# Ten ungated tiles of an up projection as five pairs in seven half-width products, and four of eleven weight sums made early

## The chip, the cores and the metric

The kernel runs on one core of a Trainium2 chip. A core has a matrix engine (TensorE, PE in the profile; its weight loads are PEld), a vector engine (VectorE, DVE), a scalar engine (ScalarE, ACT), a general one (GpSimd, POOL) and a synchronisation engine (SyncE, SP). DMA queues are fed by SP, POOL and ACT. The metric is the device time of one execution in microseconds (us), as the median of several. Profiles come from one execution of their own.

## The reference

One encoder block over 512 tokens with 1024 channels, all in float32: RMS norm, one combined projection, three token mixers (a bidirectional chunkwise mLSTM, a neighbourhood attention, a cross-attention into a memory), a gated merge, an output projection, and a feed-forward part. The change touches only the last:

```python
def conv_glu_ffn(h, w_up, w_conv, b_conv, w_down):
    a, u = jnp.split(h @ w_up, 2, axis=-1)
    return (jax.nn.gelu(dwconv3(a, w_conv, b_conv)) * u) @ w_down
```

`h` is 512 x 1024, `w_up` 1024 x 5632 (2816 columns for `a`, the gated half that goes through a convolution along the tokens and a gelu, and 2816 for `u`, the ungated half) and `w_down` 2816 x 1024.

## The kernel before

**Numbers.** A float32 product is made of three: each operand is split into a high part (a rounded copy) and a low part (the rest), and TensorE adds high x high, high x low and low x high in PSUM (`mm3`, L224 to L226). Weights arrive as blocks of 1024 columns on 128 partitions (512 KB) on SP's queue into three raw buffers (`wr`), and are split in two halves of 512: ACT copies the high part (`wh`, L184), DVE subtracts it for the low part (`wl`, L185), into four buffers each. `weights(key)` asks for a block and issues loads and splits a fixed number of blocks ahead.

**The up loop.** Channels lie on partitions, tokens along the free axis. There are 22 gated tiles (`ua`, 128 channels each) and 22 ungated ones (`uu`); each is 8 x 3 matmuls of 128 x 512 (`proj`, eight slices of 128 input channels), and tile f's two follow one another. After `ua` ACT and DVE make the convolution and the gelu (L1573 to L1576; L1574 and L1575 are 511 columns on DVE), and after `uu` DVE multiplies the two into a buffer for the down projection (L1581). The tokens' operands are `HH` (high) and `HL` (low).

**The down projection** multiplies 2 x 2 blocks with seven products in place of eight (a Strassen scheme in Winograd's form, p1 to p7, in the order of `ORDER`). It needs sums of the four weight blocks. They are made for 11 slices during the up loop, by f=2, 3, 4, 6 and on up to 15 (`SUMS`): a slice of four blocks (1 MB, `wdn`) is loaded by POOL's queue (L1477), DVE adds 1024 columns (L1495) and 512 (L1483), ACT copies 1024 (L1484), DVE adds 512 (L1492) and subtracts 1024 (L1487), and POOL's queue stores the results (`tsp`, `tdn`) to DRAM, from where the down projection loads them as its weights. From f=4 on three of a slice's four steps are issued for each f. The tokens' sums and differences for the scheme are made by `early` and `operand` (differences on DVE, a high copy on ACT, a low part on DVE, 1024 columns each).

**Order.** The kernel is written in one sequence; a framework then schedules the instructions and gives each engine its own fixed order, which the engine keeps. A wait at one instruction so holds all behind it on that engine. PSUM has buffers of one bank (`mmps`) and in the later stages wide ones of two banks (`w2p`).

The middle stages (mixers, merge, output projection) are untouched. Before them stand the projections `mlq`, `mlk` and `tm`, with convolutions on DVE (L468 to L472).

Of the kernel before, what the change touches and what calls it, by code (L numbers as in the profile page):

```python
# [17 lines left out]
P = 128  # L18
S = 512
# [12 lines left out]
NU = 15  # L32
WARM = 14
# [31 lines left out]
def block_list():  # L65

    L = []
    for i in range(4):
        L.append((("mlq", i), 1024))
    for f in range(4):  # L70
        L.append((("mlk", f), 1024))
    for c in range(3):
        for h in range(8 // TMK[c]):
            L.append((("tm", c, h), TMK[c] * TMC[c]))
    for n in ("xaq", "o", "memk", "memv", "naq", "nak"):
        for f in range(4):
            L.append(((n, f), 1024))
    for br in range(3):
        for fp in range(4):
            for f in (2 * fp, 2 * fp + 1) if br < 2 else range(8 if fp == 0 else 0):  # L80
                L.append((("g", br, f), 1024))
            L.append((("br", br, fp), 1024))
    for f in range(FT):
        L.append((("ua", f), 1024))
        L.append((("uu", f), 1024))
    return L
# [9 lines left out]
BCOLS = {n: (lambda k: P) for n in ("mlk", "o", "xaq", "memk", "naq", "nak", "g", "ua", "uu")}  # L96
BCOLS.update({n: (lambda k: 512) for n in ("mlq", "memv")})
# [5 lines left out]
def hybrid_block(ctx, tc, xg, xT, xtok, memT, wflat, wout, wdn, vecs, gbias, nabias, out):  # L103
# [64 lines left out]
    def emit_split(i):  # L168
        key, n = BLOCKS[i]
        r = raws.pop(i)  # L170
# [31 lines left out]
    def weights(key):  # L202

        i, _, n = BINDEX[key]
        calls[0] += i >= BINDEX[("naq", 0)][0]
        if calls[0] % 2 and sums:
            sums.pop(0)()
        ahead_to(i + RAW_AHEAD, i + SPLIT_AHEAD)
        return split.pop(i)

    def sum_ops():
        for dst, src, more in ((T1, wout[B11], B12), (T3, wout[B12], B22), (T2, tout[T1], B22), (T4, tout[T2], B21)):
            for add in (False, True):
# [7 lines left out]
                yield one  # L221

# [1152 lines left out]
    HH, HL = [], []  # L1375
    halves_ = (slice(0, HS), slice(HS, S))
    first.close()
    w2p = ctx.enter_context(tc.tile_pool(name="w2p", bufs=2, space=bass.MemoryType.PSUM))
# [3 lines left out]

    def pair():
        w = wide()
        return [w[:, :S], w[:, S:]]
# [17 lines left out]
    def features():  # L1403
        h2 = [unit(F32R) for _ in range(4)]
# [3 lines left out]
    def turn(i):  # L1408
        banks = [mmps() for _ in range(4)] if i == 0 else pair() + pair()
# [60 lines left out]

    down_sums = []

    def sum_load(k):
        w = unit()[:, :4 * S]
        w4 = w.rearrange("p (q n) -> p q n", q=4)
        ks = slice(k * S, (k + 1) * S)
        G.dma_start(w4, wdn[:, :, ks].rearrange("q p n -> p q n"))  # L1477
        q = [w[:, i * S:(i + 1) * S] for i in range(4)]
        hl = []

        def high():
            hl.append(unit(F32R)[:, :4 * S].rearrange("p (x q n) -> p x q n", x=2, q=2))
            V.tensor_tensor(q[B22], q[B22], q[B11], op=ALU.add)  # L1483
            A.activation(hl[0][:, 0], w4[:, 1:3], AF.Copy)  # L1484

        def low():
            V.tensor_tensor(hl[0][:, 1], w4[:, 1:3], hl[0][:, 0].bitcast(F32), op=ALU.subtract)  # L1487
            for x in range(2):
                G.dma_start(tsp[:, x, :, ks].rearrange("q p n -> p q n"), hl[0][:, x])  # L1489

        def store():
            V.tensor_tensor(q[B21], q[B21], q[B22], op=ALU.add)  # L1492
            G.dma_start(tdn[:, :, ks].rearrange("q p n -> p q n"), w4[:, 0:4:3])

        down_sums.extend([lambda: V.tensor_tensor(w[:, :2 * S], w[:, S:3 * S], w[:, :2 * S], op=ALU.add), high, store, low])  # L1495


# [57 lines left out]
    SUMS = [2 + 4 * k // 3 for k in range(HF)]  # L1555
    for f in range(FT):
# [3 lines left out]
        ur = uu_[i][j // 4][:, j % 4 * S:(j % 4 + 1) * S]  # L1560
# [11 lines left out]
        c = scr()  # L1572
        A.activation(c, pa, AF.Identity, scale=vcol("ffw", FT + f), bias=vcol("ffb", f))  # L1573
        V.scalar_tensor_tensor(c[:, 1:], pa[:, :S - 1], vcol("ffw", f), c[:, 1:], op0=ALU.mult, op1=ALU.add)  # L1574
        V.scalar_tensor_tensor(c[:, :S - 1], pa[:, 1:], vcol("ffw", 2 * FT + f), c[:, :S - 1], op0=ALU.mult, op1=ALU.add)  # L1575
        A.activation(c, c, AF.Gelu_apprx_tanh)  # L1576
# [64 lines left out]
    for name in ORDER:  # L1641
        banks[name] = [mmps(), mmps()] if name in ("p6", "p3", "p4") else pair()
# [59 lines left out]
def _layout(inp):  # L1702
# [14 lines left out]
    for key, n in BLOCKS:  # L1717
# [25 lines left out]
        elif kind == "ua":  # L1743
            b = wu[:, :, key[1] * P:(key[1] + 1) * P]
        else:
            b = wu[:, :, DFF + key[1] * P:DFF + (key[1] + 1) * P]
# [52 lines left out]
```

## Time and profile before

| what | us |
|---|---|
| median of the runs (3) | 857.08 |
| lowest and highest | 856.96, 857.18 |
| the profiled execution's own time | 857.81 |
| its span, first to last instruction | 856.0 |
| PE busy | 848.5 |
| DVE busy | 622.5 |
| ACT busy | 481.2 |
| POOL busy | 133.0 |

The span is what the trace shows; the execution's own time has 1.8 us more around it. Busy time is a sum over the span, and an engine with a small share can still be late at one place. The up loop lies from about 504 to 745 us in this trace, the stage of `mlq`, `mlk` and `tm` between 5 and 60 us or so. A row of the timeline gives start, duration, engine, line, operation, output and inputs, and shape; matmuls overlap, so their pace is read from start to start.

### The profile page before, as it was taken

What the parts mean: (1) busy time and instruction counts of PE and PEld (TensorE: products, weight loads), DVE (VectorE), ACT (ScalarE), POOL (GpSimd) and SP (SyncE); (2) the same over time, 40 slices, a digit from 0 to 9 for tenths busy, and PEclk for the clock granted to TensorE, in tenths of its full rate; (3) what the DMA queues carried; (4) which work ended last, traced back from release to release, by engine and by line L of the source; (5) the groups of instructions that cost most, each with busy time, mean ns of one, the idle gap of its engine ahead of it and who ended that gap; (6) DMA issues with size and microseconds to landing.
All of it is one profiled execution on the core that took longest, in us unless ns stands there. A gap on an engine that the chain in (4) does not pass through costs nothing.

```text
span 856.0 us, 12111 instructions
## 1 busy us (share of the span) xinstructions
PE 848.5 (99%) x4175; PEld 717.3 (84%) x4175; DVE 622.5 (73%) x1277; ACT 481.2 (56%) x989; POOL 133.0 (16%) x245
## 2 busy tenths in 40 slices
PE   9999999999999999999999999999999999999996
PEld 7898889988888888888888888888888888888885
DVE  7774698987568758898769967475758666694684
ACT  7663467675446658888735764343444444463463
POOL 0101100010127561600000111030213100011101
PEclk9999999999999999999999999999999999999999
DMA  7233542495674444543452844487869672477942
GB/s 281 80 111 121 185 153 85 158 281 163 179 202 120 115 125 127 158 144 128 144 186 98 225 144 156 153 293 261 265 222 348 208 231 99 135 258 258 380 161 100
DMA packets 53982, 155.00 MB, mean 181 GB/s; under 512 B 6872, under 2 KB 11992, under 8 KB 53344
## 3 DMA queue, kind: packets, MB, share of 16 engines
q1 hardware_dynamic: 30912, 101.37, 34.5%
q0 software_dynamic: 22576, 52.46, 20.8%
q8 instruction: 33, 0.54, 0.3%
q10 hardware_dynamic: 432, 0.39, 0.1%
q14 instruction: 29, 0.24, 0.1%
HBM read 132.68 MB, written 29.90 MB: 190 GB/s over the span
## 4 chain that ended last, share of the span: by engine, by line
PE 99%; DVE 0%; ACT 0%; POOLq 0%; issue 0%
PE mm L224 25%; PE mm L225 25%; PE mm L226 25%; PE at L225 6%; PE at L224 6%; PE at L226 6%; PE at L990 1%; PE at L971 1%; PE at L952 0%; PE at L953 0%; PE at L773 0%; PE at L821 0%; PE at L1078 0%; PE at L253 0%; PE mm L432 0%; PE mm L846 0%
## 5 line engine op out<-in xcount | busy, mean ns | idle before, releaser
L224 PE MATMUL mm<-u,wh 128*128 128x512 f32 (+1 forms) x859 | 330.2, 385 | 0.1
L225 PE MATMUL mm<-u,wh 128*128 128x512 f32 (+1 forms) x859 | 327.8, 382 | 0.0
L226 PE MATMUL mm<-u,wl 128*128 128x512 f32 (+1 forms) x859 | 327.7, 382 | 0.0
L184 ACT ACTIVATE wh<-wr 128x512 fp32r<-128x512 f32 (+2 forms) x240 | 149.7, 628 | 233.9 <-PE mm L225 199.8
L185 DVE TENSOR_TENSOR wl<-wr,wh 128x512 fp32r<-128x512 f32 (+2 forms) x242 | 164.1, 683 | 85.5 <-ACT wh L184 85.0
L226 PEld LDWEIGHTS mm<-u,wl 128*128 128x128 f32 x859 | 161.4, 188 | 31.5
L225 PEld LDWEIGHTS mm<-u,wh 128*128 128x128 f32 x859 | 161.6, 188 | 30.3 <-DVE u L231 0.4
L224 PEld LDWEIGHTS mm<-u,wh 128*128 128x128 f32 x859 | 161.4, 188 | 30.2 <-ACT u L230 0.4
L548 POOL DMA_DIRECT2D u<-nav_d x128 | 62.8, 534 | 56.2 <-PE at L990 23.4
L1132 ACT ACTIVATE u<-u 128x1024 fp32r<-128x1024 f32 (+1 forms) x28 | 27.5, 998 | 32.6 <-PE mm L226 9.0
L225 PE MATMUL at<-wl,u 128*128 128x512 f32 (+2 forms) x130 | 44.0, 339 | 0.0
L226 PE MATMUL at<-wh,u 128*128 128x512 f32 (+2 forms) x130 | 43.8, 337 | 0.0
L224 PE MATMUL at<-wh,u 128*128 128x512 f32 (+2 forms) x130 | 43.7, 337 | 0.0
L1134 DVE TENSOR_TENSOR u<-u,u 128x1024 fp32r<-128x1024 f32 (+1 forms) x21 | 23.7, 1134 | 13.6 <-ACT u L1132 13.5
L1581 DVE TENSOR_TENSOR u<-mm,s 128x512 f32<-128x512 f32 x22 | 15.2, 690 | 25.1 <-PE mm L226 23.6
L225 PE MATMUL mm<-wl,u 128*128 128x512 f32 x80 | 31.5, 394 | 0.0
L224 PE MATMUL at<-u,u 128*128 128x512 f32 x80 | 31.2, 390 | 0.0
L226 PE MATMUL mm<-wh,u 128*128 128x512 f32 x80 | 31.2, 390 | 0.0
L226 PE MATMUL at<-u,u 128*128 128x512 f32 x80 | 31.1, 389 | 0.0
L225 PE MATMUL at<-u,u 128*128 128x512 f32 x80 | 31.1, 389 | 0.0
L224 PE MATMUL mm<-wh,u 128*128 128x512 f32 x80 | 31.0, 390 | 0.0
L1489 POOL DMA_DIRECT2D tsp<-u x22 | 15.6, 709 | 96.7 <-ACT u L1484 90.1
(366 smaller groups left out, 1335.2 us busy)
## 6 DMA issues: line engine op xcount, KB each, us to landing
wr<-wflat SPq DMA_DIRECT2D x117, 512.0 KB, 3.6
u<-wdn POOLq DMA_DIRECT2D x11, 1024.0 KB, 8.2
tsp<-u POOLq DMA_DIRECT2D x22, 512.0 KB, 6.7
u<-tsp POOLq DMA_DIRECT2D x10, 1024.0 KB, 6.0
tdn<-u POOLq DMA_DIRECT2D x11, 512.0 KB, 5.7
tout<-wout POOLq DMA_DIRECT2D x4, 1024.0 KB, 10.2
nab<-nabias SPq DMA_DIRECT2D x16, 256.0 KB, 2.8
u<-nav_d POOLq DMA_DIRECT2D x128, 32.0 KB, 2.7
```

Of the source, the lines that this page charges most:

```text
L184: A.activation(h[:, u:v], src, AF.Copy)
L185: V.tensor_tensor(l[:, u:v], src, h[:, u:v].bitcast(F32), op=ALU.subtract)
L224: PE.matmul(ps, lh, rh, start=start, stop=False)
L225: PE.matmul(ps, lh, rl, start=False, stop=False)
L226: st["mm"] = PE.matmul(ps, ll, rh, start=False, stop=stop).ins
L548: G.dma_start(vw[r * 32:(r + 1) * 32, i * 256:(i + 1) * 256], nav_v[hf, r, CW[b]:CW[b] + 32, hp * 256:(hp + 1) * 256])
L971: PE.transpose(pt[:, j * P:(j + 1) * P], sm[:, j * P:(j + 1) * P], ident)
L990: PE.matmul(py[:, bl * 256:(bl + 1) * 256], vw[:, c:c + P], pp[bl][:, hf * 256:(hf + 1) * 256], start=hf == 0, stop=hf == 1)
L1132: st["oh"] = A.activation(r3(h), src, AF.Copy, scale=scale).ins
L1134: V.tensor_tensor(r3(l), src, r3(h).bitcast(F32), op=ALU.subtract)
L1489: G.dma_start(tsp[:, x, :, ks].rearrange("q p n -> p q n"), hl[0][:, x])
L1581: V.tensor_tensor(ur, pu, c, op=ALU.mult)
```

## The change

**Pairs.** For f = 2, 4, 6, 8 and 10 the ungated tiles f and f+1 become one product of 2 x 2 blocks: two halves of the input channels, two tiles of output channels, two halves of the tokens (256). Seven products of 4 x 3 matmuls of 128 x 256 take the place of 2 x 24 matmuls of 128 x 512. The weight blocks `uu` of a pair are laid out again on the host as X and Y, which are loaded but not split; DVE makes three sums of them (T, L1620, 1024 columns; p6 and p4, L1621 and L1622), and seven pieces of 512 are split (`piece`, L1630 on ACT, L1631 on DVE). The products' order is p1, p6, p7, p5, p2, p4, p3, two in one PSUM bank (`lone`). ACT and DVE put them together (L1649 to L1662), and two multiplications with the gelus give the pair's tiles.

**Operands.** The scheme needs four sums of the tokens (p5, p6, p3, p7), made once, behind tiles f=0 and f=1 (`PREP`): two sums of 2048 columns that join high and low parts (`whole`, L1581), then `early` and `operand`.

**Down sums.** Slices 0 to 3 are loaded on SP's queue in the stage of `mlk` and `tm` (behind the newest weight block), two of a slice's steps being issued at each call of `weights`; the other seven are loaded at f = 12, 13, 14, 15, 17, 18 and 19, and all four steps are issued at the next f.

```diff
+PAIRS = range(2, 12, 2)
+SUM_AT = (12, 13, 14, 15, 17, 18, 19)
...
+        if i < BINDEX[("xaq", 0)][0]:
+            for fn in down_sums[:2]:
+                down_sums.pop(0)()
+            if i in EARLY:
+                sum_load(EARLY[i], True)
...
+    EARLY = {BINDEX[key][0]: k for k, key in enumerate((("mlk", 0), ("mlk", 3), ("tm", 0, 1), ("tm", 1, 1)))}
...
+    def whole(i):
+        au.append(unit())
+        V.tensor_tensor(au[i][:, :4 * S], h2[2 * i][:, :4 * S].bitcast(F32), h2[2 * i + 1][:, :4 * S].bitcast(F32), op=ALU.add)
+    PREP = {0: (lambda: whole(0), lambda: whole(1), lambda: early(quads(au, 4), 0), lambda: sums_of_tokens("p5")),
+            1: (lambda: early(quads(au, 4), 1), lambda: sums_of_tokens("p6"), lambda: sums_of_tokens("p3"),
+                lambda: sums_of_tokens("p7"))}
...
+    def up_pair(f):
+        ur = [place(f), place(f + 1)]
+        i0 = BINDEX[("ua", f)][0]
+        c = [gelu(f, proj(("ua", f), HH, HL))]
+        X, Y = raws.pop(i0 + 2), raws.pop(i0 + 3)
...
+        V.tensor_tensor(T2, X2, Y[:, :S].unsqueeze(1).to_broadcast([P, 2, S]), op=ALU.add)
+        V.tensor_tensor(t["p6"], t["p5"], t["p3"], op=ALU.add)
+        V.tensor_tensor(t["p4"], t["p6"], t["p2"], op=ALU.add)
+        names = ("p1", "p6", "p7", "p5", "p2", "p4", "p3")
...
+                A.activation(h, t[names[n]], AF.Copy)
+                V.tensor_tensor(l, t[names[n]], h.bitcast(F32), op=ALU.subtract)
...
+        piece(0)
+        piece(1)
+        c.append(gelu(f + 1, proj(("ua", f + 1), HH, HL, at={3: lambda: piece(2), 7: lambda: piece(3)})))
...
+        for n, name in enumerate(names):
+            if n % 2 == 0:
+                b = lone()
+            ps = b[:, halves_[n % 2]]
+            wh, wl = w[name]
+            for k in range(4):
+                ks = slice(k * P, (k + 1) * P)
+                mm3(ps, wh[:, ks], wl[:, ks], *moving(name, k), k == 0, k == 3)
+            piece(n + 4)
+            if name == "p6":
+                A.activation(qa[:, lo], b[:, lo], AF.Copy)
+                V.tensor_tensor(qb[:, lo], b[:, hi], qa[:, lo], op=ALU.add)
...
-        if f in SUMS:
-            sum_load(SUMS.index(f))
-        if f >= 4:
-            for _ in range(3):
-                if down_sums:
-                    down_sums.pop(0)()
+        for fn in PREP.get(f, ()):
+            fn()
+        for fn in down_sums[:4]:
+            down_sums.pop(0)()
+        if f in SUM_AT:
+            sum_load(len(EARLY) + SUM_AT.index(f))
```

Between the early stage and the up loop DVE's order is as before. Places where it is not, in the up loop and in the early stage, are shown here. On DVE, from the product of tile f=0 on, before (`mm` are PSUM tiles, `s` scratch, `u` units of 2112 columns):

```order
L1581 TENSOR_TENSOR u_5563<-mm_5577,s_5708 128x512
L185 TENSOR_TENSOR wl_5757<-wr_5566,wh_5756 128x512
L185 TENSOR_TENSOR wl_5761<-wr_5566,wh_5760 128x512
L1574 SCALAR_TENSOR_TENSOR s_5749<-mm_5724,vec,s_5749 128x511
L1575 SCALAR_TENSOR_TENSOR s_5749<-mm_5724,vec,s_5749 128x511
```

and now:

```order
L1687 TENSOR_TENSOR u_5611<-mm_5625,s_5758 128x512
L1581 TENSOR_TENSOR u_5764<-u_5525,u_5526 128x2048
L1581 TENSOR_TENSOR u_5766<-u_5527,u_5528 128x2048
L1599 SCALAR_TENSOR_TENSOR s_5807<-mm_5782,vec,s_5807 128x511
L1166 TENSOR_TENSOR u_5764<-u_5764,u_5766 128x4x256
L1600 SCALAR_TENSOR_TENSOR s_5807<-mm_5782,vec,s_5807 128x511
L194 TENSOR_TENSOR wl_5815<-wr_5614,wh_5814 128x512
L1181 TENSOR_TENSOR u_5769<-u_5764,u_5769 128x1024
```

The two sums of 2048 and the first of the operands stand ahead of the next splits. Further on the row reaches the first pair's second piece, p6 (`wl_5909`):

```order
L1177 TENSOR_TENSOR u_5764<-u_5766,u_5764 128x4x256
L1599 SCALAR_TENSOR_TENSOR s_5895<-mm_5870,vec,s_5895 128x511
L1631 TENSOR_TENSOR wl_5905<-wr_5812,wh_5904 128x512
L1181 TENSOR_TENSOR u_5852<-u_5764,u_5852 128x1024
L1181 TENSOR_TENSOR u_5857<-u_5764,u_5857 128x1024
L1600 SCALAR_TENSOR_TENSOR s_5895<-mm_5870,vec,s_5895 128x511
L1620 TENSOR_TENSOR u_5900<-wr_5812,wr_5860 128x1024
L1599 SCALAR_TENSOR_TENSOR s_5947<-mm_5914,vec,s_5947 128x511
L1621 TENSOR_TENSOR u_5900<-u_5900,wr_5812 128x512
L1600 SCALAR_TENSOR_TENSOR s_5947<-mm_5914,vec,s_5947 128x511
L1622 TENSOR_TENSOR u_5900<-u_5900,wr_5860 128x512
L1631 TENSOR_TENSOR wl_5909<-u_5900,wh_5908 128x512
```

It has 27 instructions in all from L1687 of f=0 to this one, and the operands of p3 and p7 and T, p6 and p4 all stand ahead of it. On PE the same piece is first used here, in the last matmuls of p1 and the first of p6 (`at_5954`) and p7 (`at_5989`):

```order
L271 MATMUL at_5954<-u_5525,wh_5904 128x256
L272 MATMUL at_5954<-u_5526,wh_5904 128x256
L273 MATMUL at_5954<-u_5525,wl_5905 128x256
L271 MATMUL at_5954<-u_5849,wh_5908 128x256
L272 MATMUL at_5954<-u_5849,wh_5908 128x256
L271 MATMUL at_5989<-u_5857,wh_5927 128x256
L272 MATMUL at_5989<-u_5857,wh_5927 128x256
L273 MATMUL at_5954<-u_5849,wl_5909 128x256
```

Four matmuls that need no low part of p6 stand between p1's end and the first that does. In the early stage, the piece of DVE's difference ahead of the first `tm` block (`wl_540` and `wl_544` before, `wl_551` and `wl_555` now; `u_387` holds the first slice of `wdn`), before:

```order
L468 TENSOR_TENSOR pad_143<-at_160,rb_x 128x512
L185 TENSOR_TENSOR wl_540<-wr_426,wh_539 128x544
L185 TENSOR_TENSOR wl_544<-wr_426,wh_543 128x544
L471 SCALAR_TENSOR_TENSOR s_485<-pad_140,vec,s_485 128x512
L471 SCALAR_TENSOR_TENSOR s_491<-pad_143,vec,s_491 128x512
```

and now, where the first slice's last two steps follow the split of the block ahead:

```order
L194 TENSOR_TENSOR wl_509<-wr_377,wh_508 128x512
L263 TENSOR_TENSOR u_387<-u_387 128x512
L258 TENSOR_TENSOR u_439<-u_387,u_439 128x1024
L518 SCALAR_TENSOR_TENSOR s_479<-pad_140,vec,s_479 128x512
L518 SCALAR_TENSOR_TENSOR s_485<-pad_143,vec,s_485 128x512
```

and three rows further on, where the `tm` block's two low parts come:

```order
L515 TENSOR_TENSOR pad_143<-at_160,rb_x 128x512
L194 TENSOR_TENSOR wl_551<-wr_428,wh_550 128x544
L518 SCALAR_TENSOR_TENSOR s_491<-pad_140,vec,s_491 128x512
L518 SCALAR_TENSOR_TENSOR s_497<-pad_143,vec,s_497 128x512
L519 SCALAR_TENSOR_TENSOR s_491<-pad_140,vec,s_491 128x512
L519 SCALAR_TENSOR_TENSOR s_497<-pad_143,vec,s_497 128x512
L515 TENSOR_TENSOR pad_140<-mm_517,rb_x 128x512
L194 TENSOR_TENSOR wl_555<-wr_428,wh_554 128x544
```

The first slice's last two steps stand ahead of a convolution, and the second low part of the `tm` block, which followed the first directly, stands behind four more convolution terms and an addition.

More of the change, by code (lines that the diff above doesn't have):

```diff
@@ L221, in sum_ops, with sum_load, high, low @@
                 yield one
+    down_sums = []
+    def sum_load(k, tied=False):
+        w = unit()[:, :4 * S]
+        w4 = w.rearrange("p (q n) -> p q n", q=4)
+        ks = slice(k * S, (k + 1) * S)
+        src = wdn[:, :, ks].rearrange("q p n -> p q n")
+        if tied:
+            with tc.issue_after(st["sy"]):
+                SY.dma_start(w4, src)
+        else:
+            G.dma_start(w4, src)
+        q = [w[:, i * S:(i + 1) * S] for i in range(4)]
+        hl = []
+        def high():
+            hl.append(unit(F32R)[:, :4 * S].rearrange("p (x q n) -> p x q n", x=2, q=2))
+            V.tensor_tensor(q[B22], q[B22], q[B11], op=ALU.add)
+            A.activation(hl[0][:, 0], w4[:, 1:3], AF.Copy)
+        def low():
+            V.tensor_tensor(hl[0][:, 1], w4[:, 1:3], hl[0][:, 0].bitcast(F32), op=ALU.subtract)
+            for x in range(2):
+                G.dma_start(tsp[:, x, :, ks].rearrange("q p n -> p q n"), hl[0][:, x])
+        def store():
+            V.tensor_tensor(q[B21], q[B21], q[B22], op=ALU.add)
+            G.dma_start(tdn[:, :, ks].rearrange("q p n -> p q n"), w4[:, 0:4:3])
+        down_sums.extend([lambda: V.tensor_tensor(w[:, :2 * S], w[:, S:3 * S], w[:, :2 * S], op=ALU.add), high, store, low])
+    EARLY = {BINDEX[key][0]: k for k, key in enumerate((("mlk", 0), ("mlk", 3), ("tm", 0, 1), ("tm", 1, 1)))}
     def mm3(ps, lh, ll, rh, rl, start, stop):
@@ L1403, in features @@
     def features():
-        h2 = [unit(F32R) for _ in range(4)]
+        h2.extend(unit(F32R) for _ in range(4))
         HH.extend(h2[k // 4 * 2][:, (k % 4) * S:(k % 4 + 1) * S] for k in range(KT))
@@ L1408, in turn @@
     def turn(i):
-        banks = [mmps() for _ in range(4)] if i == 0 else pair() + pair()
+        banks = [mmps() for _ in range(4)] if i == 0 else [lone() for _ in range(4)]
         for kp in range(4):
@@ L1561, in hybrid_block @@
+    for f in range(FT):
+        if f in PAIRS:
+            up_pair(f)
+            continue
+        if f - 1 in PAIRS:
+            continue
+        ur = place(f)
         if f == 0:
```

100 lines of the change are left out of this document (64 added, 36 removed).

## The prediction

> **What bounds the kernel now.** I read the page's shares, its chain of waits and its clock row first.
>
> ```profile
> span 856.0 us, 12111 instructions
> PE 848.5 (99%) x4175; PEld 717.3 (84%) x4175; DVE 622.5 (73%) x1277; ACT 481.2 (56%) x989; POOL 133.0 (16%) x245
> PEclk9999999999999999999999999999999999999999
> PE 99%; DVE 0%; ACT 0%; POOLq 0%; issue 0%
> PE at L253 <- PEq L1792: 0.8, 1, 0.8
> ```
>
> TensorE is the bound from end to end: the chain that ended last is 99% PE, the clock was granted in full in every slice, and the list of PE's waits (last line) holds one wait, at the start. So the time is the sum of the matmuls' steps. An edit pays only by fewer or shorter steps, and any operand that comes late is paid in full: no gap is there to swallow it. Where operands come from (DVE and ACT) the mean share says little, so I read three stretches: the early projections, then the first tiles of the up loop (one row for each 10.9 us tile), then four steady ones.
>
> ```profile
> 20.00:60.00 40.00, 40.00 (x219) 35.07 (x218) 31.58 (x58) 25.04 (x40) 2.67 (x8) 1.00 0.29 103
> 60.00:100.00 40.00, 40.00 (x226) 35.16 (x226) 19.13 (x55) 17.82 (x34) 4.99 (x9) 1.00 0.50 157
> 515.00:525.90 10.90, 10.90 (x50) 9.01 (x49) 7.79 (x12) 5.65 (x10) 0.00 (x0) 1.00 0.42 146
> 525.90:536.80 10.90, 10.90 (x50) 9.02 (x49) 8.21 (x12) 3.74 (x7) 2.19 (x3) 1.00 0.62 214
> 536.80:547.70 10.90, 10.90 (x50) 9.03 (x49) 4.84 (x7) 3.74 (x7) 0.00 (x0) 1.00 0.47 171
> ```
>
> The columns are length, then busy time (and count) of PE, PEld, DVE, ACT and POOL, then clock, DMA share and GB/s. PE is full in all. DVE (third busy figure) has 2.7 to 6.1 us free in each of the tiles f=1 to 3, but only 8.4 of 40 us in the early stretch.
>
> **The change part by part.** *The pairs.* Steps are start to start:
>
> ```profile
> 560.36 0.39 PE L226 MATMUL mm<-u,wl 128*128 128x512 f32 x1
> ...
> 571.91 0.39 PE L226 MATMUL mm<-u,wl 128*128 128x512 f32 x1
> 844.99 0.28 PE L224 MATMUL mm<-u,u 128*128 128x256 f32 x1
> ...
> 848.82 0.28 PE L226 MATMUL mm<-u,u 128*128 128x256 f32 x1
> ```
>
> 51 steps of 512 columns lie between the first two: 11.55/51 = 0.2265 us. 32 steps of 256 columns lie between the other two: 3.83/32 = 0.120 us, more than half of 0.2265. Two ungated tiles are 48 steps, 48 x 0.2265 = 10.87 us; seven products are 7 x 4 x 3 = 84 steps, 84 x 0.120 = 10.08 us. A pair saves 0.79 us and five save **-3.95**. The arithmetic falls by an eighth; the narrow step eats nearly half of that.
>
> The Trainium skill ("TensorE: Matmul & The Clock Gate", Part 2: What happens when you issue a matmul) gives an isolated step of N/2.4 + 2.5 ns. An estimate by it is 109 ns for 256 columns and 216 for 512, so a pair would save 1.2 us and five 6.0. The trace's 120 and 226.5 ns disagree with it, and the measurement decides.
>
> *DVE ahead of the first pair.* This is where I expect the change to pay. Rows of the groups and of DVE's order in time:
>
> ```profile
> L231 DVE SCALAR_TENSOR_TENSOR s<-at,s 128x256 fp32r<-128x256 f32 x16 | 6.3, 420 | 1.0 <-ACT s L230 0.4
> L1484 ACT ACTIVATE u<-u 128x1024 fp32r<-128x1024 f32 x11 | 11.3, 1045 | 0.0
> 514.73 0.75 DVE L1574 SCALAR_TENSOR_TENSOR s<-mm,vec,s 128x511 f32<-128x511 f32 x1
> 515.39 0.68 DVE L185 TENSOR_TENSOR wl<-wr,wh 128x512 fp32r<-128x512 f32 x1
> 518.77 0.69 DVE L1581 TENSOR_TENSOR u<-mm,s 128x512 f32<-128x512 f32 x1 [1.44 <-ACT s L1576]
> 528.14 1.22 DVE L1495 TENSOR_TENSOR u<-u 128x1024 f32<-128x1024 f32 x1
> 529.27 0.69 DVE L185 TENSOR_TENSOR wl<-wr,wh 128x512 fp32r<-128x512 f32 x1
> 529.88 0.68 DVE L1483 TENSOR_TENSOR u<-u 128x512 f32<-128x512 f32 x1
> ```
>
> Back to back, a 512-wide operation takes 529.88 - 529.27 = 0.61 us, a 1024-wide one 1.13, a convolution term of 511 columns 0.66. A 2048-wide one isn't in the trace: by the slope from 512 to 1024 it is 1.13 + 2 x 0.52 = 2.17. The low parts of the first pair's second product, p6, now stand behind these on DVE, counted from the product of f=0 (the anchor, 518.77): ten of 512 (6.1), six convolution terms (3.96), nine of 1024 (10.17: the token operands' differences and low parts, and the pair's first weight sum) and two of 2048 (4.34). That is 27 instructions, 24.6 us, and the row of p6's low part ends at 518.77 + 24.6 = 543.4. I looked for waits inside it: the copies on ACT (1.05 us for 1024 in the second row) and the products of ua1, uu1, ua2 and ua3 are all ready when their row comes up, the tightest by 0.1 us, so the row of work is unbroken and cannot be shortened by cover.
>
> TensorE wants it earlier. ua1 starts at 515.00:
>
> ```profile
> 515.00 0.40 PE L224 MATMUL mm<-u,wh 128*128 128x512 f32 x1
> ```
>
> Four tiles of 24 steps (ua1, uu1, ua2, ua3) are 21.74, and 0.1 goes to ua2's first low part, which now ends at 526.8, where four steps of other groups cover up to 526.8: so 536.85. p1's twelve steps end at 538.3. What can be done without p6's low part is four steps (0.48), and even those wait for p6's high part: its sum ends on DVE at 541.5 and ACT's copy at 542.1. Then TensorE waits again to 543.4. Lost: 543.4 - 538.3 - 0.48 = 4.6, with ua2's 0.1 **+4.7**. From there the later products' low parts come every 0.61 us against 1.44 us of matmuls each, so nothing is lost behind it. Bounds: 4.2 if each boundary between unlike operations costs less than I take (27 x 0.02), 6 if the two 2048-wide operations cost 10% more and one ACT copy is late by 0.5.
>
> *The other pairs.* A pair takes two gated tiles and 10.08, 20.95 us. DVE's work in it: T 1.13, four convolution terms 2.64, two sums 1.22, seven low parts and four of the gated tiles' 6.7, and eight output operations (two 512-wide sums, two multiplications, one of 512 from PSUM, three of 256 at about the first row's 0.42) 4.3 to 4.6: about 16.5 of 20.95. In order of the rows p6's low part comes some 5 us ahead of need. Taken 0; 0 to 1 for all four. If this cover were gone, it would be the first pair's loss four times over.
>
> *Four down sums early.* They take DVE and ACT work out of f=4 to 12, where nobody waited: gain 0. They put 3.5 us per sum (1.13 + 0.61 + 0.61 + 1.13) into the 20 to 60 us stretch:
>
> ```profile
> 28.59 0.69 DVE L185 TENSOR_TENSOR wl<-wr,wh 128x512 fp32r<-128x512 f32 x1 [1.99 <-ACT wh L184]
> 30.68 0.69 DVE L185 TENSOR_TENSOR wl<-wr,wh 128x512 fp32r<-128x512 f32 x1 [1.40 <-ACT wh L184]
> 45.41 1.35 DVE L185 TENSOR_TENSOR wl<-wr,wh 128x544 fp32r<-128x544 f32 x2
> 47.28 1.46 DVE L471 SCALAR_TENSOR_TENSOR s<-pad,vec,s 128x512 f32<-128x512 f32 x2 [0.51 <-ACT s L470]
> 48.58 0.28 PE L224 MATMUL at<-wh,u 128*128 128x272 f32 x1
> ...
> 50.95 0.28 PE L225 MATMUL at<-wl,u 128*128 128x272 f32 x1
> wr<-wflat SPq DMA_DIRECT2D x117, 512.0 KB, 3.6
> u<-wdn POOLq DMA_DIRECT2D x11, 1024.0 KB, 8.2
> ```
>
> The first sum's first addition stands behind the split that ran at 28.59 and fits into the 1.40 us that DVE sat idle there, if its 1 MB lands by 29.5; the load is now on SP's queue at about 24, between two weight blocks. The three that follow (0.61, 0.61, 1.13) have no gap: DVE runs on from 30.7 almost without a break, so it is 2.35 us late where the tm blocks begin. The first tm tile's second low part, which ran in the x2 row at 45.41, now stands behind four more convolution terms and an addition: 45.41 + 0.61 + 2.35 + 3.9 = 52.3. TensorE begins the tile at 48.58, does 28 steps without it (19 steps lie between its two rows, 0.125 each, so 3.5) and wants it at 52.05: about 0.3, and a copy on ACT behind the same convolution is late by as much. I take **+0.5**. Bounds: 0 if the load lands early enough to shift all three into the idle 1.99 and 1.40; 2.7 if it takes 8.2 us in full behind the two weight blocks beside it and blocks DVE. The second to fourth sums lie in and behind DVE's 20.9 free us of the next 40. What queues behind the moved loads on SP are weight blocks three ahead of use: 0.
>
> *Seven sums later.* They now run at f=12 to 20. POOL issues the last load behind the stores of the sixth, some 16 us before the low parts that stand behind its additions are due. Landings:
>
> ```profile
> DMA to landing us min/median/max: 5.7/8.2/14.2
> ```
>
> By the rows on DVE there is a stall only when the last load takes over 9.8 us: 0 at the median, 4.4 at the maximum. I take **+0.3**.
>
> *The clock.* If TensorE idles as long as I say, does its clock hold? The only idle stretch of a busy TensorE in the trace is the end:
>
> ```profile
> 849.18 0.28 PE L226 MATMUL mm<-u,u 128*128 128x256 f32 x1
> 851.50:852.00 0.50, 0.00 (x0) 0.00 (x0) 0.49 (x1) 0.47 (x1) 0.00 (x0) 1.00 0.00 0
> 852.00:852.50 0.50, 0.00 (x0) 0.00 (x0) 0.00 (x0) 0.00 (x0) 0.00 (x0) 0.59 0.00 0
> 852.50:853.00 0.50, 0.00 (x0) 0.00 (x0) 0.00 (x0) 0.00 (x0) 0.00 (x0) 0.50 0.28 102
> 0.78 3.15 PE L253 MATMUL at<-const-bfloat16-1.0 128*128 128x256 bf16 x14 [0.78 <-PEq L1792]
> 5.70 0.40 PE L225 MATMUL mm<-u,wh 128*128 128x512 f32 x1
> ```
>
> The last matmul ended at 849.46 and the granted clock was halved from about 852.1, 2.6 us later. At the start 256-column matmuls take 3.15/14 = 0.225 us and the full pace is there from about 5.7, so half speed lasts up to 4.9 us of work. The new gap is 3.8 us, then 0.5 of work, then 0.8. So the clock probably drops, and returns between 544.6 and 547: 0.6 to 2.4 us lost. I take **+1.5** where it drops (60%), 0 where not.
>
> The Trainium skill ("TensorE: Matmul & The Clock Gate", Part 1: The HAM clock gate) has a free-running window of 3.4 us and halves the clock after one whole idle window. An estimate by it: a 3.8 us gap holds a whole window only one time in nine, so this would make the no-drop case the likely one, 1.5 us less. The trace's 2.6 us fits a stricter gate; I go by the trace.
>
> **Sum**: -3.95 + 4.7 + 0.5 + 0.3 + 1.5 = +3.05. The profiled execution took 857.81 us for its span of 856.0, 0.73 over the median of the runs; the difference goes onto the median: 857.08 + 3.05 = 860.1, and 858.6 without the clock's drop. Forecast: 860.0, slower by 0.34%.
>
> **Rivals.** *A: the first pair is covered* and the saving stands: 857.08 - 3.95 = 853.1, with the small terms 853.9. It needs p6's low part by 538.9, 20.1 us after the anchor instead of 24.6. For it: DVE has 8.9 us free in the three tiles ahead (the window rows), and a row of 27 leaves room for an error in what I added. Against: even with the two 2048-wide sums free (-4.34) the row ends at 539.1, no sooner than needed. 12%.
>
> *B: the stall without the clock* (the drop comes in only after a longer gap): 858.6, with a stall of 4.2 to 5.5 between 858.1 and 859.4. For it: half a us of matmuls splits the gap. 26%.
>
> *C: late loads on top.* The early load lands 8.2 us after its issue (+2.2 over what I took) and the last load at 11 to 14 (+1 to 4), with the clock as in the forecast: 862 to 864. For it: the 14.2 us landing in the row above. Against: the median is 8.2, and 512 KB weight blocks land in 3.6 us at the median (row among those of the early stretch). 14%.
>
> *D: every pair is bound by DVE*, where each pair pays 1 us or more: above 863. Against: 16.5 of 20.95. 2%.
>
> **How the numbers follow.** The forecast has 46%: stall, clock drop, small terms, 858.9 to 861.5. A measurement of this kernel tells about 0.2%, 1.71 us, from no change: same is 855.4 to 858.8. A gives faster: 0.12. Same: two thirds of B and a tenth of the forecast, 0.22. Slower: the rest, 0.66. The range 857.0 to 863.0 leaves out A below and half of C and D above, 2 in 10; the likeliest case alone is 858.9 to 861.5.
>
> **What would show each step.** In the changed profile: p1's last matmul near 538.3 and TensorE idle until about 542.1, waiting for ACT's copy of p6 and then for DVE's row (the pair's split line) near 543.4, with DVE without a gap from 518.8; a clock row below 1.00 in 540 to 547; later pairs 20.9 to 21.0 us apart with no PE wait; 84 steps of 0.120; near 52 a wait of under 1 us for a low part; up to 0.5 us near the end of the up loop. I am wrong if the wait at the first pair is under 2 us, if the clock stays at 1.00, or if later pairs wait as well.

## The result, and the profile after

The changed kernel takes 864.11 us (863.57 to 865.63, four runs) against 857.02 (856.69 to 857.18, four runs): ratio 1.0085, 95% interval 1.0072 to 1.0098. It is slower by 7.1 us, 0.85%. I had said slower, 860.0, range 857.0 to 863.0: the sign was right, the size less than half of what came, and the time lies outside the range. The profiled execution, whose trace follows, took 865.63, the longest of the four.

From the page of the changed kernel, and its list of TensorE's waits (total, times, longest), which had one line before:

```profile
span 863.8 us, 12597 instructions
PE 848.4 (98%) x4355; PEld 725.8 (84%) x4355; DVE 665.3 (77%) x1342; ACT 496.4 (57%) x1018; POOL 130.9 (15%) x241
PE at L271 <- ACT wh L1630: 3.6, 1, 3.6
PE at L272 <- DVE wl L1557: 2.0, 1, 2.0
PE mm L272 <- DVE wl L194: 1.4, 1, 1.4
PE at L300 <- PEq L1902: 0.8, 1, 0.8
PE mm L271 <- ACT wh L193: 0.6, 1, 0.6
PE at L273 <- DVE wl L1631: 0.2, 1, 0.2
```

There are four places, not one. To price each I went through the matmuls' starts and added up by how much each step exceeds 0.0133 us + columns/2400, a straight line through the two steps of the prediction (0.2266 for 512, 0.120 for 256), wherever it exceeds that by over 0.06; this counts slow clock as well as waits. Before, it gives 8.6 us, after 19.9. Each row is us lost in a stretch of the profiled execution:

| where | before | after | forecast |
|---|---|---|---|
| tm block, at 52 us | 0 | 0.9 | 0.5 for the whole early stage |
| behind the fourth early load, at 78 us | 0 | 1.6 | 0 |
| ahead of and in the first tile of the up loop, 500 to 515 us | 1.6 | 0.6 | not seen |
| first pair, 540 to 549 us | 0 | 6.1 | 6.2 (4.7 wait, 1.5 clock) |
| end of the up loop, 750 to 757 us | 0 | 3.9 | 0.3 |

**The first pair** is as forecast. DVE's row from the product of f=0 to p6's low part, and TensorE at the gap (timelines of DVE and of PE, and the window with the clock as the fraction after the counts):

```profile
520.63 0.69 DVE L1687 TENSOR_TENSOR u<-mm,s 128x512 f32<-128x512 f32 x1 [1.44 <-ACT s L1601]
521.24 4.48 DVE L1581 TENSOR_TENSOR u<-u,u 128x2048 f32<-128x2048 f32 x2
...
544.02 0.68 DVE L1622 TENSOR_TENSOR u<-u,wr 128x512 f32<-128x512 f32 x1
544.62 1.89 DVE L1631 TENSOR_TENSOR wl<-u,wh 128x512 fp32r<-128x512 f32 x3
```

```profile
540.26 0.28 PE L273 MATMUL at<-u,wl 128*128 128x256 f32 x1
544.16 0.38 PE L271 MATMUL at<-u,wh 128*128 128x256 f32 x1 [3.62 <-ACT wh L1630]
...
545.36 0.39 PE L273 MATMUL at<-u,wl 128*128 128x256 f32 x1 [0.18 <-DVE wl L1631]
...
548.75 0.41 PE L273 MATMUL at<-u,wl 128*128 128x256 f32 x1
548.96 0.32 PE L271 MATMUL at<-u,wh 128*128 128x256 f32 x1
```

```profile
545.00:550.00 5.00, 4.82 (x28) 4.64 (x27) 3.14 (x6) 2.66 (x6) 0.00 (x0) 0.66 0.31 107
```

From 520.63 the first low part in the last DVE row is done 0.6 us into it, at 545.2: 24.6 us, the figure of the forecast, and no row between them shows an idle time. TensorE waits from 540.5 to 544.2 and again to 545.4, and then steps at 0.213 us until 548.96. The other four pairs make no PE wait.

**The end of the up loop.** Rows of DVE, of the chain of waits in that window (start, length, what), of ACT and of PE:

```profile
737.10 1.23 DVE L266 TENSOR_TENSOR u<-u 128x1024 f32<-128x1024 f32 x1 [1.51 <-DMA u<-wdn]
```

```profile
741.39 5.87 DMA tdn<-u
747.36 1.07 ACT u L1179
```

```profile
747.36 1.80 ACT L1179 ACTIVATE u<-u 128x1024 fp32r<-128x1024 f32 x2 [3.67 <-DMA tdn<-u]
749.06 0.62 ACT L1601 ACTIVATE s<-s 128x512 f32<-128x512 f32 x1
749.58 0.61 ACT L1556 ACTIVATE wh<-wr 128x512 fp32r<-128x512 f32 x1
```

```profile
750.58 0.39 PE L271 MATMUL at<-wh,u 128*128 128x512 f32 x1
752.94 0.50 PE L272 MATMUL at<-wl,u 128*128 128x512 f32 x1 [1.97 <-DVE wl L1557]
...
756.64 0.63 PE L273 MATMUL at<-wh,u 128*128 128x512 f32 x1
```

The last down sum is loaded by 737.0 (its load was issued at 729.9, so it took 7.1 us, under the 9.8 from which I had a stall begin). Its result is stored from the buffer it was loaded into, and that store takes 5.9 us to land. ACT's copy of the down projection's first operand writes the same buffer of the rotating pool and waits 3.67 us for it; behind it on ACT stand the gelu of f=21 and the weights' copies, behind these DVE's products and low parts, and TensorE is idle for 2.0 us. Then it steps 512 columns at 0.43 us to 757.

**The early stage.** At the tm block, rows of ACT and of PE:

```profile
52.49 0.63 ACT L193 ACTIVATE wh<-wr 128x512 fp32r<-128x512 f32 x1 [0.46 <-PE at L273]
53.17 0.50 PE L271 MATMUL mm<-wh,u 128*128 128x512 f32 x1 [0.65 <-ACT wh L193]
```

TensorE's order now has the first matmul of the next block (`mm`) in the middle of the tm block (`at`). ACT's high copy for it waits 0.46 us for a matmul of the tm block, then takes 0.63, and TensorE waits 0.65 for the copy. The tm block's own late low part ends on DVE at 52.60, about 0.2 after TensorE could have used it.

Behind the fourth load, DVE's row, TensorE's, the landing times of the four early loads, and windows there (the number ahead of the last is DMA's share):

```profile
78.00 1.23 DVE L266 TENSOR_TENSOR u<-u 128x1024 f32<-128x1024 f32 x1 [5.45 <-DMA u<-wdn]
79.14 1.29 DVE L194 TENSOR_TENSOR wl<-wr,wh 128x512 fp32r<-128x512 f32 x2
```

```profile
79.89 0.50 PE L272 MATMUL mm<-wl,u 128*128 128x512 f32 x1 [1.36 <-DVE wl L194]
```

```profile
DMA to landing us min/median/max: 5.5/8.7/13.8
```

```profile
60.00:65.00 5.00, 5.00 (x32) 4.48 (x31) 5.00 (x14) 4.05 (x8) 2.16 (x3) 1.00 1.01 359
65.00:70.00 5.00, 5.00 (x24) 4.14 (x23) 3.95 (x7) 3.01 (x5) 1.48 (x3) 1.00 1.11 362
70.00:75.00 5.00, 5.00 (x24) 4.14 (x23) 2.28 (x12) 1.26 (x2) 0.69 (x1) 1.00 1.07 393
```

The fourth load was issued at 64.2 and landed 13.8 us later, while all 16 DMA engines were busy (a sum moves 1 MB in and 1.5 MB out beside the weight blocks). DVE idled, with the splits of the next weight block behind the waiting addition.

### The profile page after: what moved, and what is told of

Same layout as the page of the kernel before. It is cut to its first block, busy times and chain, and to the rows that moved or that the text cites. A ratio compares the mean times of both kernels' runs of the same rounds, so it can differ in the third digit from the quotient of the medians.

```text
span 863.8 us, 12597 instructions
## 1 busy us (share of the span) xinstructions
PE 848.4 (98%) x4355; PEld 725.8 (84%) x4355; DVE 665.3 (77%) x1342; ACT 496.4 (57%) x1018; POOL 130.9 (15%) x241
## 4 chain that ended last, share of the span: by engine, by line
PE 85%; DVE 5%; issue 4%; DMA 3%; POOL 1%; ACT 1%; POOLq 0%; ACTq 0%; DVEq 0%; SPq 0%
PE mm L271 19%; PE mm L272 19%; PE mm L273 19%; PE at L273 7%; PE at L272 7%; PE at L271 7%; DMA u<-wdn 3%; DVE wl L194 1%; PE at L1037 1%; PE at L1018 1%; DVE u L1181 1%; DMA tdn<-u 1%; DVE u L1581 1%; PE at L999 0%; PE at L1000 0%
## 5 line engine op out<-in xcount | busy, mean ns | idle before, releaser
L271 PE MATMUL mm<-u,wh 128*128 128x512 f32 (+1 forms) x779 | 299.7, 385 | 0.0
L272 PE MATMUL mm<-u,wh 128*128 128x512 f32 (+1 forms) x779 | 296.8, 381 | 0.0
L273 PE MATMUL mm<-u,wl 128*128 128x512 f32 (+1 forms) x779 | 296.7, 381 | 0.0
L193 ACT ACTIVATE wh<-wr 128x512 fp32r<-128x512 f32 (+2 forms) x220 | 136.8, 627 | 172.6 <-PE mm L272 124.6
L194 DVE TENSOR_TENSOR wl<-wr,wh 128x512 fp32r<-128x512 f32 (+2 forms) x222 | 150.2, 682 | 47.6 <-ACT wh L193 46.5
L273 PEld LDWEIGHTS mm<-u,wl 128*128 128x128 f32 x779 | 146.5, 188 | 28.6 <-DVE wl L194 0.3
L271 PEld LDWEIGHTS mm<-u,wh 128*128 128x128 f32 x779 | 146.8, 188 | 26.8 <-ACT u L277 0.2
L272 PEld LDWEIGHTS mm<-u,wh 128*128 128x128 f32 x779 | 146.8, 188 | 26.7
L271 PE MATMUL at<-u,wh 128*128 128x256 f32 (+1 forms) x154 | 45.9, 298 | 3.6 <-ACT wh L1630 3.6
L273 PE MATMUL at<-u,wl 128*128 128x256 f32 (+1 forms) x154 | 45.8, 298 | 0.2 <-DVE wl L1631 0.2
L272 PE MATMUL at<-u,wh 128*128 128x256 f32 (+1 forms) x154 | 45.7, 297 | 0.0
L271 PEld LDWEIGHTS at<-u,wh 128*128 128x128 f32 x154 | 30.2, 196 | 4.8 <-ACT wh L1630 4.0
L271 PE MATMUL at<-u,u 128*128 128x512 f32 x80 | 31.2, 390 | 0.0
```

Of the source, the lines that this page charges most:

```text
L193: A.activation(h[:, u:v], src, AF.Copy)
L194: V.tensor_tensor(l[:, u:v], src, h[:, u:v].bitcast(F32), op=ALU.subtract)
L271: PE.matmul(ps, lh, rh, start=start, stop=False)
L272: PE.matmul(ps, lh, rl, start=False, stop=False)
L273: st["mm"] = PE.matmul(ps, ll, rh, start=False, stop=stop).ins
```

## The experiments

Each was timed beside the kernel before on the same chip; where a time is called lost, it is counted as in the table above.

**No pairs, both shifts of the sums kept.**

```diff
-PAIRS = range(2, 12, 2)
+PAIRS = ()
...
-        for fn in PREP.get(f, ()):
-            fn()
```

> The early four sums and the late seven stay, the pairs and the tokens' sums are taken out (all 22 ungated tiles as before). Theory (three separate losses: 6.1 us at the first pair, 2.5 us in the early stage, 3.9 us where the last down sum's store holds a buffer): the first falls away with the 3.95 us of saving, the other two stay, so 857.0 + 2.5 + 3.9 = 863.4. Rival (the loss near the end of the up loop is there only because the pairs and their token sums hold buffers): 859.5. Rival (the early loss is noise of the DMA queues): 857 to 861.

862.04 (860.67 to 862.85) against 857.42, ratio 1.005 (1.0035 to 1.0065). The list of PE's waits:

```profile
PE at L272 <- DVE wl L1557: 2.0, 1, 2.0
PE mm L271 <- ACT wh L193: 0.6, 1, 0.6
PE mm L272 <- DVE wl L194: 0.2, 1, 0.2
```

The wait at the end of the up loop is there to the tenth without any pair (3.9 lost, clock included), and so is the one at the tm block (0.9); the one behind the fourth load cost 0.5 here. So moving the sums costs 4.6 us by itself. It is 1.4 less than the 863.4 that was expected: 1.1 less is lost behind the fourth load, and the 1.0 that goes at 500 to 515 us was not in the expectation. The rival with the pairs' buffers falls.

**The last sums sooner.**

```diff
-SUM_AT = (12, 13, 14, 15, 17, 18, 19)
+SUM_AT = (12, 13, 14, 15, 16, 17, 18)
```

> The last three of the seven late sums are loaded at f=16, 17 and 18 instead of 17, 18 and 19. Theory: the last store lands one tile pair (10.9 us) earlier, the wait of 2.1 us on DMA and the halved clock behind it (1.5 us) go: 864.1 - 3.8 = 860.3. Rival (it is the traffic of all late stores together that delays the down projection's first operands): 863 to 864.

860.70 (860.51 to 863.04), ratio 1.0043 (1.0028 to 1.0058), 860.3 expected. Nothing is lost at the end of the up loop; the 3.6 us wait at the first pair stands. One more tile of 10.9 us ahead of the operand's copy is enough cover for the store.

**Pairs one tile later.**

```diff
-PAIRS = range(2, 12, 2)
-SUM_AT = (12, 13, 14, 15, 17, 18, 19)
+PAIRS = range(3, 13, 2)
+SUM_AT = (13, 14, 15, 16, 17, 18, 19)
```

> Pairs at f=3, 5, 7, 9 and 11 instead of 2, 4, 6, 8 and 10 (late sums at 13 to 19); the tokens' sums stay behind f=0 and 1. Theory (a row of DVE work that is 4.7 us too long ahead of the first pair): one more ordinary tile gives 10.9 us with some 5 us of DVE in it, the wait of 3.8 and the slow clock behind it go, 864.1 - 6.1 = 858.0. Rival (every first weight sum of a pair is late, the later pairs only hide it): the wait stays over 2 us and the time 862 or more.

867.46 (866.46 to 868.85), ratio 1.0121 (1.0104 to 1.0137): 858.0 was expected, and the miss is in the second line of the edit. At the first pair nothing is lost any more, which was the question. But the seven sums now stand in seven tiles on end, each load behind the stores of the sum before, and 12.8 us are lost at the end of the loop:

```profile
PE at L271 <- ACT wh L1556: 5.9, 1, 5.9
PE at L272 <- DVE wl L1557: 2.5, 1, 2.5
```

```profile
746.29 1.06 ACT L1179 ACTIVATE u<-u 128x1024 fp32r<-128x1024 f32 x1 [6.17 <-DMA tdn<-u]
```

It is the same wait, ACT's operand copy for the last store, 2.5 us longer.

**The early sums spaced.**

```diff
-        if i < BINDEX[("xaq", 0)][0]:
+        if i < BINDEX[("o", 0)][0]:
...
-    EARLY = {... (("mlk", 0), ("mlk", 3), ("tm", 0, 1), ("tm", 1, 1)) ...}
+    EARLY = {... (("mlk", 0), ("tm", 0, 0), ("tm", 1, 2), ("xaq", 0)) ...}
```

> The four early sums are loaded at mlk 0, tm 0, tm 1 (third block) and xaq 0 instead of mlk 0, mlk 3, tm 0 and tm 1. Theory (the DMA engines are full between 60 and 75 us, the fourth load takes 13.8 us there and DVE's row waits for it): 1.6 to 2.5 us go, 861.6 to 862.5. Rival (it is DVE's work, not the landing, that is late): the same wait at another place, 864.

868.76 (866.80 to 870.74), ratio 1.0130 (1.0110 to 1.0151); 861.6 to 862.5 was expected. The wait at 78 us is gone, but a costlier one came. DVE's row and TensorE's list:

```profile
100.11 1.23 DVE L266 TENSOR_TENSOR u<-u 128x1024 f32<-128x1024 f32 x1 [3.78 <-DMA u<-wdn]
```

```profile
PE at L683 <- ACT lfc L674: 2.3, 1, 2.3
```

The fourth sum's first addition again waits for its load (9.4 us after its issue), now ahead of the mLSTM's running sums on DVE, for which TensorE waits at 119 us; 4.7 us are lost between 110 and 130, slow clock included, where the changed kernel lost 0.5. Both the time of the theory and that of the rival were missed. Ahead of the running sums stand the wait of 3.8 us and 3.5 us of the sum's own steps, and this run doesn't separate the two; spacing the loads didn't cure it.

**Token sums on POOL.**

```diff
-        V.tensor_tensor(au[i][:, :4 * S], h2[2 * i]...
+        G.tensor_tensor(au[i][:, :4 * S], h2[2 * i]...
```

(with the last sums sooner)

> As the run with the last sums sooner (860.7), and the two sums of 2048 columns are made by POOL, which is idle there, instead of DVE. Theory (a row of DVE work 4.7 us too long): the row is 4.3 us shorter, TensorE idles under 1 us, the clock holds: 860.7 - 6 = 854.7. Rival (POOL is slower than DVE at this, and the first operand's difference waits for it): DVE's row starts that much later, and with over 4 us for each sum nothing is won: 860 or more.

860.60 (860.24 to 861.60), ratio 1.0038 (1.0023 to 1.0053): nothing against 860.70. Rows of POOL, DVE and PE:

```profile
510.74 4.56 POOL L1581 TENSOR_TENSOR u<-u,u 128x2048 f32<-128x2048 f32 x1 [4.64 <-DVE u L278]
516.38 4.58 POOL L1581 TENSOR_TENSOR u<-u,u 128x2048 f32<-128x2048 f32 x1 [1.08 <-DVE u L278]
```

```profile
512.06 3.79 DVE L194 TENSOR_TENSOR wl<-wr,wh 128x512 fp32r<-128x512 f32 x1 [0.68 <-ACT wh L193]
517.39 4.13 DVE L194 TENSOR_TENSOR wl<-wr,wh 128x512 fp32r<-128x512 f32 x1 [1.14 <-ACT wh L193]
```

```profile
516.30 0.38 PE L272 MATMUL mm<-u,wh 128*128 128x256 f32 x1 [2.88 <-DVE u L278]
```

The rival was right in the time, for another reason. POOL takes 4.6 us for each sum and it starts early, so the operands are not late. But a split on DVE that takes 0.69 us lasts 3.79 and 4.13 beside POOL's sum, and both times it ends 0.55 us after the sum does, about its own length later; DVE's normalised tokens behind it are late, and TensorE waits 2.9 us at f=0, with the halved clock behind it. At the first pair itself 1.6 us are lost instead of the 6.7 of the run with the last sums sooner. The Trainium skill ("SBUF — State Buffer", Terms) says that the two engines arbitrate for a port pair that is held for a full instruction; the two DVE rows agree.

**Filler in the gap.** 32 matmuls of 256 columns on constants between p1 and p6 of the first pair:

```diff
+            if f == 2 and name == "p1":
+                fb = lone()
+                for _ in range(FILL):
+                    PE.matmul(fb[:, :256], one[:, :P], one, start=True, stop=True)
             piece(n + 4)
```

> The changed kernel with 32 more matmuls of 256 columns on constants between p1 and p6 of the first pair (about 3.5 us, into a bank that nobody reads), in the 3.8 us in which TensorE idles. Theory (the halved clock behind the gap comes from the idling): the wait as a whole stays, the steps of 0.213 behind it go back to 0.12: 864.1 - 1.4 = 862.7. Rival (the steps are slow because low parts and copies come late): 864.1, or more by what the filler delays.

864.39 (862.15 to 865.18), ratio 1.0076 (1.0061 to 1.0092): by the medians no gain over 864.11, and 862.7 was expected. The runs of either kernel spread by 2 to 3 us, so the medians can't tell 1.4. The traces can: the granted clock stays at 1.00 through the first pair, and beside the filler's 32 x 0.120 = 3.8 us 1.0 is lost there, 4.8 in place of 6.1. The same filler where the last sums come sooner:

> The kernel with the last sums sooner (860.7) with the same 32 filler matmuls between p1 and p6 of the first pair, where no wait at the end of the up loop blurs the comparison. Theory (the clock is halved by the idling): TensorE still does nothing useful for about 4.7 us there, but the steps behind it are 0.12 instead of 0.213: 860.7 - 1.4 = 859.3. Rival (the clock isn't the cause of the slow steps): 860.7 or more.

859.45 (858.48 to 861.66), ratio 1.0025 (1.0015 to 1.0035), against 860.70 without it; 859.3 was expected. A window of this kernel after the gap (the same window has a clock of 0.70 without the filler, and the one before it 0.62):

```profile
545.00:550.00 5.00, 5.00 (x44) 5.00 (x43) 4.13 (x7) 2.61 (x6) 0.00 (x0) 1.00 0.66 207
```

The clock holds when TensorE doesn't idle, and that is worth 1.3 us by the medians (whose ranges overlap) and 1.9 by the traces (6.7 lost against 1.0 and the filler's 3.8). Here the slow stretch that falls away was 6.8 us long, in the changed kernel it was 3.4 and worth 1.2; its 17 steps from 545.36 to 548.96 are 1.6 longer than 17 x 0.120. So 1.2 to 1.6 of the changed kernel's 6.1 us at the first pair is clock, the rest wait.

**The last store from another buffer.**

```diff
-            G.dma_start(tdn[:, :, ks]..., w4[:, 0:4:3])
+            G.dma_start(tdn[:, :, ks]..., w4[:, 0:4:3] if k < HF - 1 else hl[0][:, 0].bitcast(F32))
```

> The changed kernel, but the last down sum's third store (to tdn) reads the same amount from the buffer of the other stores instead of from the loaded slice's own buffer (so one slice of two sums is wrong in the output); loads, sums, order and bytes are as before. Theory (ACT's copy of the down projection's first operand waits for this store to land because it writes the same buffer): the 3.7 us that ACT waits go, unless the other buffer is next in line; 864.1 - 2 to 3.8 = 860.3 to 862. Rival (full DMA engines or the late load cause the wait): 864.

863.74 (861.43 to 867.06), ratio 1.0074 (1.0048 to 1.0100): the median doesn't tell it from the changed kernel. Rows of ACT:

```profile
740.30 1.06 ACT L1179 ACTIVATE u<-u 128x1024 fp32r<-128x1024 f32 x1 [0.77 <-DVE u L258]
749.04 1.06 ACT L1179 ACTIVATE u<-u 128x1024 fp32r<-128x1024 f32 x1 [2.52 <-DMA tsp<-u]
```

The first operand's copy, which waited for the store until 747.4, runs at 740.3 (this trace is 1.2 us ahead at the last load). So it was the buffer, with the same loads and bytes in flight. The wait went to the next in line, as the expectation allowed: a later copy, of another operand, writes the buffer from which the other two stores (and now the third) go out, and waits for them. TensorE still idles 1.7 us in two pieces, but its clock stays at 1.00 and 2.0 us are lost there instead of 3.9.

**Four pairs from f=3.** Late sums at f=11 to 18 with three early ones, or at 11 to 17 with four:

```diff
+PAIRS = range(3, 11, 2)
+SUM_AT = tuple(range(11, 19))
...
+    EARLY = {... (("mlk", 3), ("tm", 0, 1), ("tm", 1, 1)) ...}
```

> Four pairs at f=3, 5, 7 and 9; three early sums (mlk 3, tm 0, tm 1), eight late ones at f=11 to 18. Theory (losses at the first pair, by the first early load and by the last store all avoided): 857.2 - 4 x 0.79 + 0 to 1.0 = 854.0 to 855.0. Rival (the sums that are packed into f=11 to 18 are too dense, as in the run with the pairs one later): 858 or more.

> The same four pairs with the four early sums of the changed kernel and seven late ones at f=11 to 17. Theory: what the early stage costs by itself (0.9 at the tm blocks, 0.5 to 1.6 behind the fourth load) on top of the saving: 857.2 - 3.16 + 1.4 to 2.5 = 855.4 to 856.5. Rival (the early stage's loss depends on the late sums or the pairs): equal to the run with three early sums.

856.15 (855.43 to 856.77), ratio 0.9982 (0.9973 to 0.9992), with three; 856.90 (856.13 to 857.83), ratio 0.9993 (0.9984 to 1.0002), with four. Without the first early sum nothing is lost at 52 us, with it 0.9. They came out 1.2 and 0.4 us above the upper ends of what was expected: with three, 1.0 is lost behind the last early load, and in both waits of 0.3 to 0.4 for the down projection's weights (`u<-tsp`) show near 782 us, with 1.8 and 2.1 lost between 775 and 850 where the kernel before loses 0.5.

**p3's operand later.** Five pairs from f=2 and the last sums sooner; the last two steps of the token sums (p3's, 2 x 1.13 us; `third(1)`) moved behind the first pair's first product, the step before them (`third(0)`) left where it was:

```diff
-            1: (..., lambda: sums_of_tokens("p6"), lambda: sums_of_tokens("p3"),
-                lambda: sums_of_tokens("p7"))}
+            1: (..., lambda: sums_of_tokens("p6"), lambda: third(0),
+                lambda: sums_of_tokens("p7"))}
...
+            if n == 0 and f == PAIRS[0]:
+                third(1)
```

> Five pairs from f=2 with the last sums sooner (860.7), and the last two steps of the token sums (p3's, two operations of 1024 columns) moved behind the first pair's first product; by that two convolution terms also move behind p6. Theory (the length of DVE's row ahead of p6's low part sets the wait): the row is 2 x 1.13 + 2 x 0.66 = 3.6 us shorter, the wait 1.1 us instead of 4.7, the clock holds: 860.7 - 3.6 - 1.4 = 855.7. Rival (some other piece, such as ACT's copies, is as late): 858 or more.

855.82 (855.11 to 857.32), ratio 0.9981 (0.9972 to 0.9990); 855.7 was expected. PE's longest wait:

```profile
PE at L273 <- DVE wl L1644: 1.5, 1, 1.5
```

The wait is 1.5 us, now for p1's low part, and no clock drop follows. Shortening DVE's row by 3.6 us brought 4.9 (6.7 lost at the first pair became 1.8): the row's length sets the wait, and the wait sets the clock. The places add up too: of the 3.95 saved 0.9 goes at the tm block, 0.4 behind the fourth load and 1.8 at the first pair, 1.0 comes from 500 to 515 us, which leaves 1.9; the medians differ by 1.85.

**Four pairs, two early sums, p3's operand later.** One sum is loaded at f=1, eight at f=11 to 18, two early (mlk 3, tm 1).

> Pairs at f=3, 5, 7 and 9; two early sums (mlk 3 and tm 1), one sum loaded at f=1, eight at f=11 to 18; the last two steps of the token sums (p3's) moved behind the first pair's first product. Theory: early stage without loss (0 to 0.3), 3.5 us more DVE work before the first pair, 2.3 us less, against 1.4 us that were idle: 857.4 - 3.16 + 0.3 to 1.3 = 854.5 to 855.5. Rival (the loads at 780 to 830 us are what is left and stay): 856.1.

854.89 (854.22 to 856.10) against 857.67, ratio 0.9970 (0.9958 to 0.9981), within the 854.5 to 855.5 that were expected. This is the best of the study, 2.8 us under the kernel before and 9 under the change as made. Its list of waits is nearly empty again:

```profile
PE at L300 <- PEq L1917: 0.8, 1, 0.8
PE at L272 <- DVE wl L1557: 0.2, 1, 0.2
```

Four pairs save 4 x 0.79 = 3.2 us, and 2.8 arrive by the medians. The 2.8 is not the pairs' alone: 1.0 comes from 500 to 515 us, and 0.6 more than before is lost between 775 and 850.

## Why the prediction was right and wrong

**Right: the saving.** In the changed kernel the 84 steps of each of the four later pairs take 10.07 us, where the sum had 10.08: the steps of 0.120 us for 256 columns held. With the waits out of the way the total agrees too, 2.8 us by the medians with four pairs, of 3.2, though other stretches gain and lose some tenths beside it.

**Right: the first pair.** The row of 27 instructions took the 24.6 us that were forecast, 6.1 us are lost there against 6.2, and the later pairs have no wait. The run with p3's operand later shows the row as the cause, and the two runs with the filler the clock's share, 1.2 to 1.6 against 1.5. None of the three things that were to show the prediction wrong came. The sign that failed is "up to 0.5 us near the end of the up loop", where TensorE waited 2.0. Rival A needed the row to be covered, and it isn't; B needed the clock to hold over a 3.8 us gap, and it doesn't.

**Wrong: "Seven sums later", taken +0.3, measured 3.9.** The step asked when the load lands. The load took 7.1 us, inside the 9.8, though DVE waited 1.5 us for it; what TensorE's operands waited for was the store at the other end, because its source buffer is the next that ACT writes. I had followed what waits for the sum's result and not who gets its buffer. Neither that nor a clock that drops a second time was in the bound of 4.4, which hung on a slow load; that the bound is of the right size is chance.

**Wrong: "Four down sums early", taken +0.5, measured 2.5 in the profiled execution.** Two parts. The tm block lost 0.9 where I had 0.3 and a copy as late: the low part was some 0.2 late, near the 0.3. But TensorE's order now has the next block's first matmul inside the tm block, and ACT's copy for it, which has the late convolution ahead of it until 52.03, then waits 0.46 more for a matmul of the tm block. The step had the place right, and was undersized. What failed outright is the sentence that the second to fourth sums lie in DVE's 20.9 free us of the next 40. I counted DVE's time and not the landing: while DVE waits for 1 MB in its fixed order, its free time is of no use to the splits behind. The loss follows the landing in the ten traces with these four loads in place: nothing where the fourth took up to 12.2 us (four runs), 0.2 to 0.5 at 12.4 to 12.7 (five), 1.6 at 13.8 (the changed kernel). Past 12.2 us TensorE pays every microsecond. The first load, to which the bound of 2.7 belonged, cost DVE a wait of 0.7 us only. Whether the late landing also makes the changed kernel's runs spread by 2 us is not shown; runs with no wait at the end of the loop spread as much.

**Missed, in the other direction:** 1.0 us that the kernel before loses at 500 to 515 us is gone in the changed one, without pairs too. The change also gives the `ident` matmuls there (L1415 before, L1459 now) PSUM tiles of one bank (`lone`) in place of wide ones. Whether that is the reason was not tried.

Together: 6.1 + 0.9 + 1.6 + 3.9 - 1.0 = 11.5 lost, less 3.95 saved, is 7.6; the two spans differ by 7.8. Rival C, late loads on top of the forecast, had the time to 0.1 (862 to 864), in part by luck: it made the first early load and the last load late, and late were the fourth early load and the last store.

Two figures of the prediction don't come out of its rows, with no effect on the sum. By the window rows DVE has 11.9 us free in the three tiles of rival A, not 8.9 (and 5.2 between the anchor and 538.9). The terms of DVE's work in a later pair add up to 16.0 to 16.3, not 16.5; the third pair of the changed kernel shows 16.2 of 20.98.

## What to carry to other kernels

When work is moved on an engine that keeps a fixed order, follow three things for each instruction: when its input lands, how long the row ahead of the next urgent instruction gets, and which later instruction gets the buffer that it (or its store) holds. Free time of the engine tells none of them. A gap of TensorE that is long enough (2.0 us and more here) costs its length and then over a microsecond of slow clock, so several short waits are cheaper than one long one, and a change whose gain is 4 us must be placed so that none of it forms.

## What the runs showed of the hardware

- **The clock falls sooner than I had read.** 2.0 us of idling (750.97 to 752.94) were followed by half speed from about 753.8 to 757; 1.5 us (p3's operand later) and 1.7 us in two pieces (other buffer) were not. Half speed lasted 3.4 us both times in the changed kernel; behind the same gap at the first pair it was 6.8 with the last sums sooner and with the other buffer, and behind two gaps (5.9 and 2.5 us) with the pairs one later 10.2. So each was one, two or three times 3.4. The Trainium skill ("TensorE: Matmul & The Clock Gate", Part 1: The HAM clock gate) has a window of 3.4 us and one idle window as the condition: the length of the slow stretches agrees, the condition doesn't, since TensorE worked for over a third of any 3.4 us window around the 2.0 us gap.
- **POOL's sums stop DVE's.** A 128x2048 sum on POOL (4.6 us) stretched a DVE subtraction that runs alongside from 0.69 to 3.79 and 4.13 us, ending 0.55 us after the sum; nothing was won by the move (860.60 against 860.70).
